# Tile pools change sides of the on-chip memory, and the state-space outputs move into the attention

## The chip, the cores and the metric

One core of one Trainium2 chip runs the whole program. The metric is the device time of one execution in microseconds (us); before the change it is 2275.36 us, the median of three runs that lie between 2270.74 and 2281.77 us. The profile was taken in one further execution.

## The reference

Two transformer blocks on 512 tokens of width 1024, all in float32. The first block has two layers. Layer 0 mixes with a windowed attention over the 512 tokens and 256 context tokens, layer 1 with a gated linear attention (GLA); each is followed by an MLP, `square(relu(h @ w_in)) @ w_out` with 4096 hidden columns. The second block projects `h` to q, k, v, a state-space input u and 2048 gate columns, and adds two branches:

```
gate   = sigmoid(proj[..., 3*D_ATTN+D_SSM:] + b_gate)
y_attn = chunked_relpos_attention(q, k, v, ...)        # 8 heads, causal within the 512 tokens
y_ssm  = s5_ssm_glu(u, ...)                            # scan; y = C s + D u; z = gelu(y)
                                                       # z * sigmoid(z @ w_glu + b_glu)
merged = gate[:, :, 0] * (y_attn @ wb[:D_ATTN]) + gate[:, :, 1] * (y_ssm @ wb[D_ATTN:])
x = x + merged @ w_out
x = x + hierarchical_moe(rms_norm(x), ...)             # 16 experts, top 2
```

## The kernel before, in words

**Products.** A float32 product is made of three float32r matmuls: each operand is split into a high part (a rounded copy, by ScalarE) and a rest (a subtraction, by VectorE), and high x high, high x rest and rest x high are added in PSUM. `Kern.unit` (L217) loads 1 MB of weights into a tile `raw` and splits it into `whi` and `wlo` (128 x 2048 each). `mm3s` (L248 to L252) writes the three matmuls. Of a matmul's two operands one is loaded into the array (stationary, 128 columns) and the other is streamed through it, here mostly 512 columns.

- `inproj` (L250 and its neighbours with `hl` in the profile's names): the weights are stationary, the activations `h` (high and rest, 16 KB per partition each) are streamed.
- The second half of `mlp` (`second`, names `hid`): the hidden activations are stationary, `whi` (lines L248 and L252) and `wlo` (L250) are streamed.
- `out_full` (names `oh`, `ol`): the weights are streamed, two units of them from `whi`/`wlo`, two from tiles `wr` of its own.

One MLP has 16 blocks of 256 hidden columns; each block has an `inproj` of 2 x 8 x 3 matmuls for each group of tokens, and a second part of 4 x 3 matmuls for each tile of 128 tokens. Layer 0 has a group of 512 tokens (`hl`) and one of 256 (`hc`), which alternate matmul by matmul; layer 1 has the 512 alone, and its first two blocks are cut into halves of 256 columns.

**Where tiles lie.** Pools are taken from two stacks: the left one grows upward from 16.1 KB of a partition's 224 KB, the right one downward from 224 KB. `Kern.left` and `Kern.right` go through `K.sides`, which can exchange the two. Before, the left stack begins with the constants (4.9 KB), the pool `wstream` (2 x `raw`, 2 x `whi`, 2 x `wlo`, 48 KB) and small scalars (1.1 KB). In the built program this puts `raw` at 21 to 37 KB, `whi` at 37 to 53 KB, `wlo` at 53 to 69 KB, the residual `X` at 70 to 86 KB, the MLPs' `hl` at 86 to 118 KB, and the block 2 input `h4` (its tiles are called `hl` too) at 127 to 159 KB. The hidden activations lie between 147 and 199 KB. In layer 0's `out_full`, `oh` and `ol` lie at 122 to 138 KB and `wr` at 138 to 170 KB.

**Order.** The Tile framework places each engine's instructions with a simulated timeline; the order in which the program emits them is its priority. In block 2 the emission is a set of Python generators (`block2_mix`, L1440): `scores(h)` yields after each of the four score tiles of a head, and at every second of these 32 steps one half of a gate unit (`gate_unit`, 24 matmuls with `h4` streamed, 16 halves in all) is emitted. `values` (the transposes of p and the products with V) of two heads follow during the next two heads. After the attention come, in this order: the loads of eight gate tiles, `ssm.load` (matrices G and W3, 2 MB each, W3 cut from DRAM in eight strided pieces), the first branch product (`ya`, 96 matmuls), in which `ssm.outputs` is emitted at two places, the GLU product (`z`, 48 matmuls), and the second branch product (`ys`). `ssm.outputs(Q)` computes a half of the state-space outputs: 16 matmuls with G and W3 for each of four `ii`, two copies, eight transposes, a gelu.

Of the kernel before, what the change touches and what calls it, by code (L numbers as in the profile page):

```python
# [19 lines left out]
P = 128  # L20
# [130 lines left out]
class Kern:  # L151
    def __init__(self, tc, A, at):
        self.tc, self.nc, self.A, self.at = tc, tc.nc, A, at
        self.stack = ExitStack()
        e = self.stack.enter_context
        self.c = e(tc.tile_pool(name="const", bufs=1))
        self.w = e(tc.tile_pool(name="wstream", bufs=2))
        self.s = None
        self.t = e(tc.tile_pool(name="tiny", bufs=6))
        self.dram = e(tc.tile_pool(name="dram", bufs=1, space=bass.MemoryType.DRAM))  # L160
        self.p2 = e(tc.tile_pool(name="ps2", bufs=2, space=bass.MemoryType.PSUM))
        self.p1 = e(tc.tile_pool(name="ps1", bufs=4, space=bass.MemoryType.PSUM))
        nc = self.nc


        self.ident = self.c.tile([P, P], F32, name="ident")
        self.identb = self.c.tile([P, P], BF, name="identb")
        self.csil = self.c.tile([P, KC, 32], F32, name="csil")
        self.small = self.c.tile([P, A["small"].shape[1]], F32, name="small")
        nc.sync.dma_start(self.small, A["small"])  # L170
        make_identity(nc, self.ident)
        nc.vector.tensor_copy(self.identb, self.ident)
        self.n = 0
        self.norms = []
        self.sides = {"left": "left", "right": "right"}
        edge = e(tc.tile_pool(name="edge", bufs=1, side="right"))
        self.mhalf = edge.tile([P, 8], F32, name="mhalf")
        self.edge_aff = edge.tile([P, 2, KC], F32, name="edge_aff")
        nc.vector.memset(self.mhalf, -0.5)
# [11 lines left out]

    def scratch(self, side="right"):

        st = ExitStack()
        self.s = st.enter_context(self.tc.tile_pool(name="scratch", bufs=1, side=side))
        return st
# [20 lines left out]
    def unit(self, ap, r=None, to=None, after=None, pool=False):  # L217

        r = self.raw(ap) if r is None else r
        hi, lo = to or (self.w.tile([P, 2048], F32R, tag="w" + x, name=self.nm("w" + x)) for x in ("hi", "lo"))  # L220
        ins = self.nc.scalar.copy(hi, r).ins  # L221
# [299 lines left out]
def layer0_attn(K):  # L521
# [11 lines left out]
    with ExitStack() as left:  # L533
        qp = left.enter_context(tc.tile_pool(name="qkv", bufs=1))
        Q = [qp.tile([P, NCTX + L], F32R, name=K.nm("Q")) for _ in range(16)]
# [301 lines left out]
def layer0(K):  # L837
# [26 lines left out]
    with K.scratch(), K.right("gate") as gp:  # L864
# [15 lines left out]
        mw, mw_close = K.opened(K.left("mw"))  # L880
        mlp(K, 0, list(h), [4, 2], finish2, swap, "right", filler=K.mod_dots(gp, mw), steps=4)
    K.ctx_close.close()
# [267 lines left out]
def layer1(K, X, h, ssm):  # L1150
# [16 lines left out]
    with K.scratch(), K.right("gate") as gp:  # L1167
# [13 lines left out]
        tp, t_close = K.opened(K.left("ssmt"))  # L1181
        mlp(K, 1, [h3], [4], finish2, swap, "right", True, ssm.constants(tp))
    return h


class SSM:


    def __init__(self, K):
        self.K = K  # L1190
        self.w1 = K.dram.tile([P, 2, 16, P], F32, name="ssm_w1")
        self.g = K.dram.tile([P, 2, 16, P], F32, name="ssm_g")
        self.k = K.dram.tile([16, 32, 15, 16], F32, name="ssm_k")
        self.a8 = K.c.tile([P, 2, 2, 16], F32, name="ssm_a8")

    def constants(self, tp):
# [149 lines left out]
        for q in range(8):  # L1346
            nc.gpsimd.dma_start(self.k.rearrange("c (a q) l x -> q c a (l x)", q=8)[q][:, :, 7 * 16:],
                                kk[16 * q:16 * q + 16])

    def inputs(self, zp, sp, u_rows):  # L1350

# [46 lines left out]

    def load(self, sp, between):

        nc = self.K.nc
        self.G = sp.tile([P, 2, 16, P], F32, name="ssm_g2", bufs=1)
        self.W3 = sp.tile([P, 32, P], F32, name="ssm_w3", bufs=1)
        for part in range(2):
            nc.sync.dma_start(self.G[:, part], self.g[:, part])
        between()
        for t in range(8):
            nc.sync.dma_start(self.W3[16 * t:16 * t + 16].rearrange("p g (t c) -> p g t c", t=8),
                              self.k[:, :, 7 - t:15 - t, :])

    def outputs(self, sp, Q, zT):

        K, Z, UT, G, W3 = self.K, self.Z, self.UT, self.G, self.W3
        nc, a, mm = K.nc, K.nc.scalar, K.nc.tensor.matmul
        b = [K.bank() for _ in range(2)]
        for ii in range(4):
# [8 lines left out]
            for g in range(2):  # L1425
                for i, o in os:
                    mm(o[g], UT[:, 2 * i + g, :], W3[:, 2 * i + g, :],
                       start=False, stop=True, skip_group_check=True)
        Y = sp.tile([P, 8, P], F32, tag="ssm_y", name=K.nm("Y"), bufs=1)
        for g, e in enumerate((a.copy, K.nc.vector.tensor_copy)):  # L1430
            e(Y.rearrange("p t (i g c) -> p g t i c", g=2, c=16)[:, g],
              b[g].rearrange("p (i t c) -> p t i c", i=4, t=8))
        b = K.bank2()
        for t in range(8):
            nc.tensor.transpose(b[:, t * P:t * P + P], Y[:, t, :], K.ident)
        for h in range(2):
            a.activation(zT[:, 2 * Q + h].rearrange("p (j t) -> p t j", t=8),
                         b.rearrange("p (t h j) -> p h t j", t=8, h=2)[:, h], AF.Gelu_apprx_tanh)


def block2_mix(K, X, hl, ssm, out):
# [6 lines left out]
    with ExitStack() as left:  # L1448
# [85 lines left out]

        with K.right("at2", 2) as ap:
            def scores(h):
# [57 lines left out]

            def gates(c0, c1):
                for c in range(c0, c1):
                    yield from gate_unit(c)

            last, done, gen = iter(()), [], gates(0, 8)
            for h in range(8):  # L1600
                for n, _ in enumerate(scores(h)):
                    if n % 2:
                        next(last, None)
                    else:
                        next(gen, None)
                if h % 2:
# [8 lines left out]
        z_close.close()  # L1615

        K.h_close.close()
        K.sides = {"left": "left", "right": "right"}
        K.opool = ExitStack()
# [22 lines left out]
        zs.push(sz_close)  # L1642
        gl = zs.enter_context(K.left("ssmz", 2))
        z = K.pair(gl, "z", [P, 4, L])
# [5 lines left out]

        with K.left("ssmr", 2) as sp:
            for r in range(4):
                fetch(r)
            ssm.load(sp, lambda: [fetch(r) for r in range(4, 8)])
            for c in range(2):
                w = K.unit(A["w_br"][c])
                for m in range(4):
                    f = 4 * c + m
                    b, g = branch(w, ya, m, f, f)
                    v.tensor_mul(mT[:, f, :], b, g)  # L1660
                    if c and m in (2, 3):
                        ssm.outputs(sp, m - 2, zT)
                        turned = parts(m - 2)
        yo = left.enter_context(K.left("b2o"))
# [38 lines left out]
class Moe:  # L1703
# [259 lines left out]
    def split(self, r):  # L1963
        K = self.K
        if self.nhi < 3:
            pool = self.more if self.nhi == 2 else K.w
            self.his.append([pool.tile([P, 2048], F32R, tag=t, name=K.nm(t)) for t in ("whi", "wlo")])
        hi, lo = self.his[self.nhi % 3]
# [118 lines left out]
def program(tc, A, at, out):  # L2087
# [3 lines left out]
    h = layer1(K, X, h, ssm)  # L2091
    K.sides = {"left": "right", "right": "left"}
    block2_mix(K, X, h, ssm, out).finish(X)
# [20 lines left out]
```

## Time and profile before

| | us |
|---|---|
| median of three runs | 2275.36 |
| the profiled execution's own time | 2268.23 |
| its span | 2266.2 |
| TensorE (PE) busy | 2138.9 (94%) |
| VectorE (DVE) busy | 1390.6 (61%) |
| ScalarE (ACT) busy | 971.2 (43%) |
| GpSimd (POOL) busy | 334.8 (15%) |
| TensorE's mean granted clock | 0.976 of full |

Busy time is a union of the records of one engine. Matmuls overlap in their records, since each record holds the pipeline's latency too: what one costs in a full stream is the distance from its start to the next one's start, which the timeline shows. "Idle before" in a row is the time that the engine stood still just ahead of the instruction, with what released it.

### The profile page before, as it was taken

The numbers are of one execution on the slowest core, as the hardware profiler recorded it, in microseconds if no ns is written. First come the engines' busy times: TensorE is split into PE (matmuls) and PEld (weight loads), VectorE is DVE, ScalarE is ACT, GpSimd is POOL, SyncE is SP. The second block draws the span as 40 slices with busy tenths as digits, with TensorE's granted clock in tenths as the row PEclk, the third lists the DMA queues.
The fourth block names the chain that finished last, engine by engine and source line by source line (L and its number), as shares of the span: only waits on it lengthen the run. The fifth ranks groups of instructions, "written<-read, shape, count | busy, mean of one in ns | idle before, by whom it ended". The sixth has DMA issues, their size and how long they took to land. (4 is left out here: it accounts for less than half of the span.)

```text
span 2266.2 us, 30706 instructions
## 1 busy us (share of the span) xinstructions
PE 2138.9 (94%) x12088; PEld 1769.3 (78%) x12088; DVE 1390.6 (61%) x2436; ACT 971.2 (43%) x1512; POOL 334.8 (15%) x453
## 2 busy tenths in 40 slices
PE   7999999999999999999989999999899997897996
PEld 5876668888888888789977887888799874686875
DVE  4666654999644444631794597555646754547985
ACT  5446656421121222542554632322353453535874
POOL 0035622112000000510000000000220100012332
PEclk9999999999999999999999999999999998998998
DMA  7112231557321121211211224232322435468993
GB/s 291 64 39 98 82 149 38 195 189 255 122 75 56 56 75 56 72 38 59 93 38 38 88 93 149 106 104 84 120 94 94 154 122 115 174 237 278 331 298 105
DMA packets 57970, 279.12 MB, mean 123 GB/s; under 512 B 9248, under 2 KB 13744, under 8 KB 32992
## 3 DMA queue, kind: packets, MB, share of 16 engines
q1 hardware_dynamic: 38048, 219.39, 27.4%
q0 software_dynamic: 18768, 55.04, 7.7%
q10 hardware_dynamic: 1008, 2.70, 0.4%
q8 instruction: 96, 1.57, 0.3%
q14 instruction: 50, 0.41, 0.1%
HBM read 264.54 MB, written 24.08 MB: 127 GB/s over the span
## 5 line engine op out<-in xcount | busy, mean ns | idle before, releaser
L221 ACT CAST whi<-raw 128x2048 fp32r<-128x2048 f32 x106 | 202.4, 1909 | 559.3 <-PE b L252 389.1
L222 DVE TENSOR_TENSOR wlo<-raw,whi 128x2048 fp32r<-128x2048 f32 x106 | 246.0, 2322 | 223.4 <-ACT whi L221 222.1
L250 PE MATMUL b<-hl,whi 128*128 128x512 f32 (+1 forms) x736 | 284.1, 386 | 2.3 <-DVE t L323 1.5
L248 PE MATMUL b<-hl,whi 128*128 128x512 f32 (+1 forms) x736 | 283.0, 385 | 0.8 <-ACT whi L221 0.8
L252 PE MATMUL b<-hl,wlo 128*128 128x512 f32 (+1 forms) x736 | 281.6, 386 | 0.0
L815 DVE TENSOR_TENSOR acc<-acc,b 128x512 f32<-128x512 f32 x280 | 180.8, 682 | 156.0 <-PE b L252 155.7
L248 PE MATMUL b<-whi,hid 128*128 128x512 f32 x640 | 215.5, 395 | 2.5 <-ACT whi L221 1.9
L250 PE MATMUL b<-wlo,hid 128*128 128x512 f32 x640 | 216.8, 394 | 0.0
L252 PE MATMUL b<-whi,hid 128*128 128x512 f32 x640 | 215.1, 395 | 0.0
L250 PEld LDWEIGHTS b<-hl,whi 128*128 128x128 f32 x736 | 139.1, 189 | 30.3 <-issue 2.9
L248 PEld LDWEIGHTS b<-hl,whi 128*128 128x128 f32 x736 | 139.1, 189 | 30.1 <-ACT whi L221 1.3
L252 PEld LDWEIGHTS b<-hl,wlo 128*128 128x128 f32 x736 | 139.3, 189 | 28.3 <-issue 0.2
L1970 DVE TENSOR_TENSOR wlo<-raw,whi 128x2048 fp32r<-128x2048 f32 x57 | 129.8, 2287 | 27.7 <-ACT whi L1970 27.7
L252 PEld LDWEIGHTS b<-whi,hid 128*128 128x128 f32 x640 | 120.3, 188 | 27.9
L248 PEld LDWEIGHTS b<-whi,hid 128*128 128x128 f32 x640 | 119.2, 188 | 29.0 <-ACT whi L221 2.1
L250 PEld LDWEIGHTS b<-wlo,hid 128*128 128x128 f32 x640 | 120.5, 188 | 27.4
L1970 ACT CAST whi<-raw 128x2048 fp32r<-128x2048 f32 x57 | 108.4, 1912 | 10.7 <-PE b L242 10.6
L627 POOL TENSOR_TENSOR p<-p,t 128x512 f32<-128x512 f32 (+2 forms) x96 | 92.5, 972 | 62.8 <-DVE t L626 62.2
L402 DVE CUSTOM_DVE_ANT_0 junk<-mw,cb 128x1024 bf16<-128x1024 f32 x80 | 97.6, 1220 | 3.6 <-DMA mw<-in_w_modT_dram 2.9
L240 PE MATMUL b<-whi,hl 128*128 128x256 f32 x320 | 91.3, 285 | 2.3 <-ACT qr L1478 2.3
L241 PE MATMUL b<-wlo,hl 128*128 128x256 f32 x320 | 91.4, 286 | 0.0
L242 PE MATMUL b<-whi,hl 128*128 128x256 f32 x320 | 91.2, 285 | 0.0
(602 smaller groups left out, 4709.8 us busy)
## 6 DMA issues: line engine op xcount, KB each, us to landing
raw<-in_w_e_dram SPq DMA_DIRECT2D x57, 1024.0 KB, 7.0
raw<-in_w_mlp_in_dram SPq DMA_DIRECT2D x32, 1024.0 KB, 5.1
raw<-in_w_mlp_out_dram SPq DMA_DIRECT2D x32, 1024.0 KB, 4.7
mw<-in_w_modT_dram POOLq DMA_DIRECT2D x56, 512.0 KB, 4.5
raw<-in_w_mod_dram SPq DMA_DIRECT2D x20, 1024.0 KB, 6.3
raw<-in_w_in_dram SPq DMA_DIRECT2D x16, 1024.0 KB, 4.8
raw<-in_gla_in_dram SPq DMA_DIRECT2D x12, 1024.0 KB, 4.8
raw<-in_w_o_dram SPq DMA_DIRECT2D x8, 1024.0 KB, 4.7
```

Source lines behind the costliest of these rows:

```text
L221: ins = self.nc.scalar.copy(hi, r).ins
L222: ins = ins, (self.nc.gpsimd if pool else self.nc.vector).tensor_sub(lo, r, hi.bitcast(F32)).ins
L240: mm(out, ah, bh, start=start, stop=False)
L241: mm(out, ah, bl, start=False, stop=False)
L242: mm(out, al, bh, start=False, stop=stop)
L248: mm(o, ah, b, start=start, stop=False)
L250: mm(o, ah, b, start=False, stop=False)
L252: mm(o, al, b, start=False, stop=stop)
L402: v.tensor_tensor_reduce(junk, w, cb[b], 1.0, 0.0, ALU.mult, ALU.add, to[:, k, b:b + 1])
L627: nc.gpsimd.tensor_mul(p[:, :n], p[:, :n], den.to_broadcast([P, n]))
L815: nc.vector.tensor_add(a, a, bs[n])
L1970: ins = K.nc.scalar.copy(hi, r).ins, K.nc.vector.tensor_sub(lo, r, hi.bitcast(F32)).ins
```

## The change

The permanent pools go to the right stack in a new order, `whi` and `wlo` get pools of their own, and every `left` and `right` of the three phases is exchanged. In block 2 the state-space outputs become a generator that fills steps of the attention after the gates; the fill is advanced at every step of the scores, not at every second one. Their matrices G and W3 are loaded once the gates are done; W3 is laid out ahead in DRAM by eight GpSimd DMAs (`k8`) at the end of layer 1's preparation, so that it comes in one load. Their scratch tile Y is taken from the `whi` pool, and the transposes and gelus are cut in two. The split of `zT` (`parts`) moves to the first unit of the first branch.

```diff
@@ Kern.__init__
-        self.c = e(tc.tile_pool(name="const", bufs=1))
-        self.w = e(tc.tile_pool(name="wstream", bufs=2))
+        edge = e(tc.tile_pool(name="edge", bufs=1, side="right"))
+        self.w = e(tc.tile_pool(name="wstream", bufs=2, side="right"))
+        self.c = e(tc.tile_pool(name="const", bufs=1, side="right"))
+        self.t = e(tc.tile_pool(name="tiny", bufs=6, side="right"))
+        self.wsplit = {x: e(tc.tile_pool(name=f"w{x}", bufs=2, side="right")) for x in ("lo", "hi")}
-        self.sides = {"left": "left", "right": "right"}
+        self.sides = {"left": "right", "right": "left"}
@@ unit
-        hi, lo = to or (self.w.tile([P, 2048], F32R, tag="w" + x, name=self.nm("w" + x)) for x in ("hi", "lo"))
+        hi, lo = to or (self.wsplit[x].tile([P, 2048], F32R, tag="w" + x, name=self.nm("w" + x)) for x in ("hi", "lo"))
@@ layer0, layer1 (both calls of mlp)
-        mlp(K, 0, list(h), [4, 2], finish2, swap, "right", ...)
+        mlp(K, 0, list(h), [4, 2], finish2, swap, "left", ...)
@@ SSM.constants
+        for t in range(8):
+            nc.gpsimd.dma_start(self.k8[16 * t:16 * t + 16].rearrange("p g (t c) -> p g t c", t=8),
+                                self.k[:, :, 7 - t:15 - t, :])
@@ SSM.load
-        between()
-        for t in range(8):
-            nc.sync.dma_start(self.W3[16 * t:16 * t + 16].rearrange("p g (t c) -> p g t c", t=8),
-                              self.k[:, :, 7 - t:15 - t, :])
+        nc.sync.dma_start(self.W3, self.k8)
@@ SSM.outputs
-        b = [K.bank() for _ in range(2)]
...
+            yield
-        Y = sp.tile([P, 8, P], F32, tag="ssm_y", name=K.nm("Y"), bufs=1)
+        Y = K.wsplit["hi"].tile([P, 2048], F32, tag="whi", name=K.nm("Y"))[:, :1024].rearrange("p (t c) -> p t c", t=8)
...
+        yield
+        for x in range(2):
+            for t in range(4):
+                nc.tensor.transpose(b[x][:, t * P:t * P + P], Y[:, 4 * x + t, :], K.ident)
+            for h in range(2):
+                a.activation(zT[:, 2 * Q + h].rearrange("p (j t) -> p t j", t=8)[:, 4 * x:4 * x + 4],
+                             b[x].rearrange("p (t h j) -> p h t j", t=4, h=2)[:, h], AF.Gelu_apprx_tanh)
+        yield
@@ block2_mix
-        with K.right("at2", 2) as ap:
+        sr = ExitStack()
+
+        def ssm_outputs():
+
+            K.h_close.close()
+            ssm.load(sr.enter_context(tc.tile_pool(name="ssmr", bufs=1, side=K.sides["right"])))
+            for Q in range(2):
+                yield from ssm.outputs(gbank, Q, zT)
+
+        with K.left("at2", 2) as ap:
...
+            def fill():
+                for c in range(8):
                     yield from gate_unit(c)
+                yield from ssm_outputs()
...
                     if n % 2:
                         next(last, None)
-                    else:
-                        next(gen, None)
+                    next(gen, None)
...
-        with K.left("ssmr", 2) as sp:
-            for r in range(4):
-                fetch(r)
-            ssm.load(sp, lambda: [fetch(r) for r in range(4, 8)])
...
-                    if c and m in (2, 3):
-                        ssm.outputs(sp, m - 2, zT)
-                        turned = parts(m - 2)
+        for r in range(8):
+            fetch(r)
...
+                if c == 0 and m < 2:
+                    turned = parts(m)
@@ program
-    K.sides = {"left": "right", "right": "left"}
+    K.sides = {"left": "left", "right": "right"}
     block2_mix(K, X, h, ssm, out).finish(X)
```

## Rows read from the trace of the kernel before

**Rows 1.** The profile's page, its first line.

```profile
span 2266.2 us, 30706 instructions
```

**Rows 2.** Busy time by stretch: PE, PEld, DVE, ACT, POOL (instructions), clock, DMA share, GB/s.

```profile
395.00:1043.00 648.00, 635.46 (x3357) 543.19 (x3356) 389.40 (x565) 187.36 (x298) 69.85 (x85) 0.99 0.31 106
...
1258.00:1642.00 384.00, 372.66 (x1781) 306.81 (x1780) 251.15 (x376) 129.13 (x163) 26.56 (x32) 0.99 0.31 107
...
1755.00:1861.00 106.00, 106.00 (x500) 83.98 (x500) 71.56 (x220) 52.41 (x94) 9.68 (x22) 1.00 0.39 134
1861.00:1898.00 37.00, 30.30 (x134) 17.02 (x132) 22.19 (x69) 17.43 (x42) 0.74 (x2) 0.86 0.12 43
1898.00:1957.00 59.00, 45.26 (x326) 34.04 (x325) 17.70 (x18) 28.30 (x32) 0.00 (x0) 0.91 0.70 172
```

**Rows 3.** Groups by line and form, PE: one of three MLP second-part lines.

```profile
L250 PE MATMUL b<-wlo,hid 128*128 128x512 f32 x640 | 216.8, 394 | 0.0
```

**Rows 4.** Timeline of PE in layer 1's MLP: start us, us, instruction, count.

```profile
1326.79 0.39 PE L248 MATMUL b<-hl,whi 128*128 128x512 f32 x1
...
1333.76 0.40 PE L252 MATMUL b<-hl,wlo 128*128 128x512 f32 x1
...
1343.75 0.39 PE L248 MATMUL b<-whi,hid 128*128 128x512 f32 x1
...
1349.32 0.39 PE L250 MATMUL b<-hl,whi 128*128 128x512 f32 x1
```

**Rows 5.** Timeline of PE in block 2's gates, `h4` streamed.

```profile
1781.80 0.39 PE L252 MATMUL b<-hl,wlo 128*128 128x512 f32 x1
...
1790.19 0.39 PE L248 MATMUL b<-hl,whi 128*128 128x512 f32 x1
```

**Rows 6.** Timeline of PE in layer 0's `out_full`, one tile of tokens.

```profile
337.25 0.62 PE L252 MATMUL b<-whi,ol 128*128 128x512 f32 x2
...
341.91 0.63 PE L248 MATMUL b<-wr,oh 128*128 128x512 f32 x2
342.38 0.62 PE L250 MATMUL b<-wr,oh 128*128 128x512 f32 x2
...
347.37 0.62 PE L248 MATMUL b<-whi,oh 128*128 128x512 f32 x2
```

**Rows 7.** Timeline of PE after the attention: the state-space outputs and the waits around.

```profile
1917.84 1.12 PE L1423 MATMUL b<-ssm_g,ssm_z 64*64 64x128 f32 x8 [5.74 <-DVE mT L1660]
...
1929.15 0.66 PE L1427 MATMUL b<-ssm_w,ssm_ut 128*64 128x128 f32 x8 [4.19 <-DMA ssm_w<-ssm_k]
...
1940.63 0.66 PE L1427 MATMUL b<-ssm_w,ssm_ut 128*64 128x128 f32 x8
...
1946.69 1.03 PE L1435 MATMUL b<-ident,Y 128*128 128x128 f32 x8
...
1951.00 1.19 PE L248 MATMUL b<-z,whi 128*128 128x512 f32 x4 [1.90 <-ACT z L1648]
...
1957.42 0.73 PE L248 MATMUL b<-ys,whi 128*128 128x512 f32 x2 [0.33 <-ACT ys L1676]
```

**Rows 8.** Timeline of ACT in the attention's end and after it.

```profile
1864.48 1.27 ACT L1545 CAST KH<-kT 64x512 fp32r<-64x512 f32 x2
...
1875.84 1.24 ACT L1545 CAST KH<-kT 64x512 fp32r<-64x512 f32 x2
...
1898.05 0.59 ACT L1592 CAST ya<-b 128x512 fp32r<-128x512 f32 x1 [4.13 <-PE b L1585]
...
1916.34 0.72 ACT L1637 ACTIVATE g<-g,small 128x512 f32<-128x512 f32 x1 [9.84 <-DMA g<-gates_d]
...
1936.77 1.28 ACT L1437 ACT_TABLE_LOAD   x1
```

**Rows 9.** Timeline of POOL in layer 1's MLP.

```profile
1515.55 4.06 POOL L1347 DMA_DIRECT2D ssm_k<-ssm_kk  x8 [82.96 <-ACT hf L755]
1612.74 4.62 POOL L222 TENSOR_TENSOR ya<-raw,ya 128x2048 fp32r<-128x2048 f32 x1 [93.13 <-ACT ya L221]
```

More of the change, by code (lines that the diff above doesn't have):

```diff
@@ L155, in __init__ @@
         e = self.stack.enter_context
-        self.c = e(tc.tile_pool(name="const", bufs=1))
-        self.w = e(tc.tile_pool(name="wstream", bufs=2))
+        edge = e(tc.tile_pool(name="edge", bufs=1, side="right"))
[3 more added lines that the diff above has]
+        self.wsplit = {x: e(tc.tile_pool(name=f"w{x}", bufs=2, side="right")) for x in ("lo", "hi")}
         self.s = None
-        self.t = e(tc.tile_pool(name="tiny", bufs=6))
         self.dram = e(tc.tile_pool(name="dram", bufs=1, space=bass.MemoryType.DRAM))
@@ L174, in __init__ @@
         self.norms = []
-        self.sides = {"left": "left", "right": "right"}
-        edge = e(tc.tile_pool(name="edge", bufs=1, side="right"))
+        self.sides = {"left": "right", "right": "left"}
         self.mhalf = edge.tile([P, 8], F32, name="mhalf")
@@ L190, in opened, with scratch @@
         return st.enter_context(pool), st
-    def scratch(self, side="right"):
+    def scratch(self, side="left"):
         st = ExitStack()
@@ L533, in layer0_attn @@
     with ExitStack() as left:
-        qp = left.enter_context(tc.tile_pool(name="qkv", bufs=1))
+        qp = left.enter_context(K.left("qkv"))
         Q = [qp.tile([P, NCTX + L], F32R, name=K.nm("Q")) for _ in range(16)]
@@ L880, in layer0 @@
         mw, mw_close = K.opened(K.left("mw"))
-        mlp(K, 0, list(h), [4, 2], finish2, swap, "right", filler=K.mod_dots(gp, mw), steps=4)
+        mlp(K, 0, list(h), [4, 2], finish2, swap, "left", filler=K.mod_dots(gp, mw), steps=4)
     K.ctx_close.close()
@@ L1181, in layer1 @@
         tp, t_close = K.opened(K.left("ssmt"))
-        mlp(K, 1, [h3], [4], finish2, swap, "right", True, ssm.constants(tp))
+        mlp(K, 1, [h3], [4], finish2, swap, "left", True, ssm.constants(tp))
     return h
@@ L1193, in __init__ @@
         self.k = K.dram.tile([16, 32, 15, 16], F32, name="ssm_k")
+        self.k8 = K.dram.tile([P, 32, P], F32, name="ssm_k8")
         self.a8 = K.c.tile([P, 2, 2, 16], F32, name="ssm_a8")
@@ L1397, in ahead, with load @@
         self.us = [K.unit(W[6 + i], to=[flat(x) for x in t], pool=i == 0) for i, t in enumerate((self.ya, (zT, UT)))]
-    def load(self, sp, between):
+    def load(self, sp):
         nc = self.K.nc
@@ L1405, in load, with outputs @@
             nc.sync.dma_start(self.G[:, part], self.g[:, part])
-        between()
-        for t in range(8):
-            nc.sync.dma_start(self.W3[16 * t:16 * t + 16].rearrange("p g (t c) -> p g t c", t=8),
-                              self.k[:, :, 7 - t:15 - t, :])
-    def outputs(self, sp, Q, zT):
+        nc.sync.dma_start(self.W3, self.k8)
+    def outputs(self, b, Q, zT):
         K, Z, UT, G, W3 = self.K, self.Z, self.UT, self.G, self.W3
         nc, a, mm = K.nc, K.nc.scalar, K.nc.tensor.matmul
-        b = [K.bank() for _ in range(2)]
         for ii in range(4):
@@ L1432, in outputs @@
               b[g].rearrange("p (i t c) -> p t i c", i=4, t=8))
[L1433 to L1438, printed above, removed]
+        yield
[6 more added lines that the diff above has]
+        yield
 def block2_mix(K, X, hl, ssm, out):
@@ L1593, in values @@
                 v.tensor_sub(ya[1][:, m, :], O, ya[0][:, m, :].bitcast(F32))
-            def gates(c0, c1):
-                for c in range(c0, c1):
+            def fill():
+                for c in range(8):
                     yield from gate_unit(c)
-            last, done, gen = iter(()), [], gates(0, 8)
+                yield from ssm_outputs()
+            last, done, gen = iter(()), [], fill()
             for h in range(8):
@@ L1615, in block2_mix @@
         z_close.close()
-        K.h_close.close()
-        K.sides = {"left": "left", "right": "right"}
+        sr.close()
+        K.sides = {"left": "right", "right": "left"}
         K.opool = ExitStack()
@@ L1642, in block2_mix @@
         zs.push(sz_close)
-        gl = zs.enter_context(K.left("ssmz", 2))
+        gl = zs.enter_context(K.right("ssmz", 2))
         z = K.pair(gl, "z", [P, 4, L])
@@ L1649, in parts @@
                     v.tensor_sub(z[1][:, d], zT[:, d], z[0][:, d].bitcast(F32)).ins)
-        with K.left("ssmr", 2) as sp:
-            for r in range(4):
-                fetch(r)
-            ssm.load(sp, lambda: [fetch(r) for r in range(4, 8)])
[L1655 to L1660, printed above, removed]
-                    if c and m in (2, 3):
-                        ssm.outputs(sp, m - 2, zT)
-                        turned = parts(m - 2)
+        for r in range(8):
+            fetch(r)
+        for c in range(2):
+            w = K.unit(A["w_br"][c])
+            for m in range(4):
+                f = 4 * c + m
+                b, g = branch(w, ya, m, f, f)
+                v.tensor_mul(mT[:, f, :], b, g)
+                if c == 0 and m < 2:
+                    turned = parts(m)
         yo = left.enter_context(K.left("b2o"))
@@ L1965, in split @@
         if self.nhi < 3:
-            pool = self.more if self.nhi == 2 else K.w
-            self.his.append([pool.tile([P, 2048], F32R, tag=t, name=K.nm(t)) for t in ("whi", "wlo")])
+            self.his.append([(self.more if self.nhi == 2 else K.wsplit[t]).tile([P, 2048], F32R, tag="w" + t,
+                                                                                name=K.nm("w" + t)) for t in ("hi", "lo")])
         hi, lo = self.his[self.nhi % 3]
```

## The prediction

> **What bounds the kernel now.** The span is 2266.2 us [rows 1]; the profiled execution took 2268.23 us and the median of three runs is 2275.36, so whatever is summed here against the profile is put on the median, 7.1 us higher. I read busy time by stretch first. In both MLPs PE is busy for all but 13 of 648 and 11 of 384 us, and VectorE and the DMA queues have room: 60 to 65% busy, and a DMA share of 0.31 [rows 2]. There a time can only fall if each matmul costs less. The gates' stretch is full too: 106 of 106 us. Then PE goes loose: 30.3 us of 37 in the attention's end and 45.3 of 59 behind it, at a mean clock of 0.86 and 0.91 of full, between its two levels of 1.2 and 2.4 GHz [rows 2]. The change has one part for each kind of stretch.
>
> **Part one, the places.** A matmul's cost in a full stream is read from start to start. In layer 1's MLP 31 with `hl` streamed start in 6.97 us (30 steps, 232.3 ns) and 24 with `whi` and `wlo` streamed take 5.57 us (232.1 ns) [rows 4]. In the gates 38 with `h4` streamed start in 8.39 us (37 steps, 226.8 ns) [rows 5]. Both `hl` runs have the same shapes, the same line, and `whi`/`wlo` as the stationary operand; what differs is that `hl` lies at 86 to 118 KB and `h4` at 127 to 159 KB. The best contrast is inside one loop: in `out_full` 20 matmuls that stream `whi`/`wlo` (37 to 69 KB) take 4.66 us, 233.0 ns each, and 22 that stream `wr` (138 to 170 KB) take 4.99 us, 226.8 ns, with the same stationary tiles [rows 6]. So a 512-column matmul costs 5.5 ns less when its streamed operand lies in the upper part. Why, no row shows.
>
> The Trainium skill ("TensorE: Matmul & The Clock Gate", section "Wait — 56ns, not 53.3ns?") has the distance from start to start as the columns over 2.4 GHz plus about 2.5 ns, 215.7 ns for 512 columns, wherever the operand lies. The trace disagrees twice, in size and in the two paces; by the page part one would be worth nothing.
>
> The new places follow from the stack. From 224 KB down: `raw` 16, constants 4.9, scalars 1.1, `wlo` 16, `whi` 16, `X` 16, `hl` 32. So `wlo` lies at 186 to 202 KB, `whi` at 170 to 186, the MLPs' `hl` at 122 to 154; in block 2 `X`, 24 KB of `ya`/`zT` and 16.6 KB of state-space tiles put `h4` at 81 to 113. Terms, at 5.5 ns:
> - `whi` streamed in the MLPs' second parts: two of three lines of 640 [rows 3], 1280 x 5.5 = -7.0 us.
> - `wlo`: 640, above every place that rows 4 to 6 show as quick: between 0 and -3.5; I take -1.8.
> - Layer 1's `hl`: 16 x 2 x 8 x 3 = 768, less 192 cut into 256 columns: 576 x 5.5 = -3.2.
> - Layer 0's `hl`: 768, each followed by a 256-column one, a pair for which no row stands: 0 to -4.2; I take -1.0.
> - The gates lose their place: 16 x 24 = 384 x 5.5 = +2.1.
> - `out_full` gains for `whi` what it loses for `wr`; the experts and the branches go both ways: 0, by at most 1.5 either way (some 300 matmuls).
>
> That is -10.9; a run that is broken up need not keep the quick pace, so I take **-9**, with ends -14 and +4 (the losses alone).
>
> **Part two, the state-space outputs.** From the last head's output (1898.05) [rows 8] to the first matmul of `ys` (1957.42) [rows 7] lie 59.4 us. PE is busy for 45.3 us of them [rows 2]. What goes: the state-space matmuls, nearly all between 1929.15 and 1941.3, 12 us, 8 transposes at 1946.69 (1.0), and the waits. The 5.74 us that PE stood before 1917.84 is put down to `mT`, and that one waited for a sigmoid whose gate tile arrived only at 1916.34, 9.84 us late, its DMA between those of G and W3 [rows 8]; the 4.19 us before 1929.15 is W3 itself; the 1.90 before 1951.00 is the split of the second half of `zT` [rows 7]. So 45.3 - 13 = 32.3 us of work stay, `ya` and `z`; a mean clock of 0.91 over the stretch says that a few of these ran at 1.2 GHz, and I take 3 off. 59.4 - 29.3 = **-30 us**.
>
> What comes back in the attention:
> - Its own end. The gates now come at every step. If the scores keep to their emission, only four heads are done when the gates run out, where the trace has five, and a head without cover takes 11.4 us (the K copies of two heads at 1864.48 and 1875.84 [rows 8]); less its matmuls that moved, about +8 to +13. If the framework starts scores when they are ready, as now, 0. I take +6.
> - The 13 us of matmuls fall into idle time: 37 - 30.3 = 6.7 us [rows 2], about as much again with one more head. What doesn't fit: +3 (0 to 6).
> - Gelu stands among exponentials. One table load is 1.28 us [rows 8]; two groups of gelus give up to four more loads and spare one, 5.1 - 1.3 us on ScalarE, which is half idle: +3 (0 to 4).
> - The first branch shares its banks with the outputs and can start less early: +1 (0 to 3).
>
> The Trainium skill ("ScalarE: Activation LUTs", section "What ACT_TABLE_LOAD costs") has about 2.7 us for a load; the row has 1.28. By the page this term would be up to +8 and the sum 5 us worse.
>
> At nothing: the eight `k8` DMAs. POOL has no work between the `ssm_k` writes at 1515.55 (0.5 us each) and 1612.74, 93 us [rows 9], and 2 MB beside a DMA share of 0.31 [rows 2] delay nobody; without that cover they would cost POOL some 5 us. The loads of G and W3 start when `h4` is free and have the attention's end as cover; if that is too short, see the third rival. The moved `parts` (1 us on ACT, 1.2 on DVE each) lie beside `ya`.
>
> Sum of part two: -30 + 6 + 3 + 3 + 1 = **-17**, ends -28 and -4. Both parts: 2268.2 - 26 = 2242 on the profile, 2249 on the median.
>
> **Rivals.**
> 1. *The place counts for nothing* (the skill's rule, or a cause that only looks like a place, such as which pool was written last). For it: no row shows a mechanism. Against it: rows 6 change pace in one loop, with one stationary operand. Then only -17 is left: 2258.
> 2. *Everything falls well*: the attention ends where it did, `wlo` is quick too. -14 - 28: 2234. For it: in the trace gates and scores were not tied to their emission.
> 3. *The new operands come late*: PE takes its queue in order, so a state-space matmul that waits for G or W3 holds the scores behind it, and these the exponentials. 4 MB at the 172 GB/s of rows 2 need 24 us. Held for 12 us, part two gives -5 and the sum is 2261, or 2266 with half of part one: no change.
> 4. *Slower*: the same hold at its full 24 us, with its price added to heads that are themselves without cover (+13 and the 7 for tables and banks): -30 + 24 + 13 + 7 = +14, 2289, or 2280 if part one holds. It decides from the point at which hold and longer attention exceed the 30 us taken away, and is slower only if the places give nothing. Against it: the simulated timeline sets what it expects to be late further back in the queue.
>
> **How the numbers follow.** 0.5% is 11.4 us, about what a measurement of this kernel can tell from no change. The forecast has 0.50, the first rival 0.18, the second 0.10, the third 0.14, the fourth 0.08. Forecast and first two are faster, but a first rival with a longer attention is not (0.02 off): faster 0.76, same 0.16, slower 0.08. The range takes in the second rival's time and the third's, and leaves out the fourth: 2233 to 2271.
>
> **What would show it.** Right: in layer 1's MLP, `hl` and `whi` runs near 227 ns from start to start, and the two MLP stretches some 7 and 4 us shorter; `wlo` decides the disputed 3.5. The gates at 232. No L1423 or L1427 after the last `ya` copy, no wait of PE for `mT` or W3 there, and 27 to 32 us from that copy to the first `ys`. The last copy itself 0 to 20 us later, counted from the gates' start. Wrong: MLP runs still at 232 (first rival); a wait of L1423 or L1427 for a DMA with scores behind it (third and fourth); a PE that is idle by more than 20 us in the attention's end; or a stretch outside these that grows, since all pools have new neighbours, and a tile's first write waits for whoever lay there before.

## The result and the profile after

The changed kernel takes 2247.41 us, the median of four runs (2239.76 to 2248.39), against 2273.53 for the kernel before, the median of four (2270.74 to 2281.77): a ratio of 0.9877, with a 95% interval of 0.9858 to 0.9896. It is faster by 26 us, 1.2%. The forecast was 2249, its range 2233 to 2271. The profiled execution took 2239.76 us, span 2237.9, 28.3 less than the span of before [rows 1]; the other three runs are about 8 us longer, so its trace is used for stages only.

Busy time by stretch, with the columns of [rows 2] (PE, PEld, DVE, ACT, POOL, clock, DMA share, GB/s), of the changed kernel:

```profile
395.00:1041.00 646.00, 632.11 (x3348) 542.10 (x3349) 388.59 (x564) 185.97 (x295) 68.83 (x84) 0.99 0.31 106
1258.00:1635.00 377.00, 364.71 (x1781) 305.99 (x1780) 250.87 (x376) 129.81 (x165) 30.62 (x40) 0.99 0.33 115
...
1848.00:1908.00 60.00, 48.84 (x379) 31.26 (x378) 33.16 (x96) 38.90 (x76) 0.83 (x3) 0.97 0.32 119
1908.00:1935.00 27.00, 26.64 (x117) 21.70 (x117) 18.34 (x19) 21.07 (x26) 0.00 (x0) 1.00 0.72 254
```

The attention's end now takes 60 us where it took 37, the chain behind it 27 where it took 59, and PE's clock there is 0.97 and 1.00 where it was 0.86 and 0.91 [rows 2].

How long an MLP takes is read best from one line's first and last start: the matmuls that stream `wlo`, in layer 0's MLP (x384) and in layer 1's (x256). Instructions by line, the kernel before:

```profile
L250 PE MATMUL b<-wlo,hid x384: 390/392/479, 432.6 to 942.4; 128*128 128x512 f32 x192
...
L250 PE MATMUL b<-wlo,hid x256: 387/393/404, 1290.1 to 1632.8; 128*128 128x512 f32 x128
```

The same view of the changed kernel:

```profile
L253 PE MATMUL b<-wlo,hid x384: 387/389/478, 432.3 to 939.1; 128*128 128x512 f32 x192
...
L253 PE MATMUL b<-wlo,hid x256: 389/389/402, 1291.1 to 1626.5; 128*128 128x512 f32 x128
```

Timeline of the changed kernel: a run of `hl` and one of `whi`/`wlo` in layer 1's MLP, one tile of layer 0's `out_full`, the gates (their first matmul; then a run), the first `ys`, and the last matmuls of the program:

```profile
336.60 0.62 PE L255 MATMUL b<-whi,ol 128*128 128x512 f32 x2
...
341.13 0.62 PE L251 MATMUL b<-wr,oh 128*128 128x512 f32 x2
...
346.57 0.62 PE L251 MATMUL b<-whi,oh 128*128 128x512 f32 x2
...
1326.90 0.39 PE L251 MATMUL b<-hl,whi 128*128 128x512 f32 x1
...
1333.70 0.39 PE L255 MATMUL b<-hl,wlo 128*128 128x512 f32 x1
1333.93 1.07 PE L251 MATMUL b<-whi,hid 128*128 128x512 f32 x4
...
1339.37 0.39 PE L251 MATMUL b<-hl,whi 128*128 128x512 f32 x1
...
1747.13 0.39 PE L251 MATMUL b<-hl,whi 128*128 128x512 f32 x1
...
1774.13 0.39 PE L255 MATMUL b<-hl,wlo 128*128 128x512 f32 x1
...
1781.10 0.39 PE L255 MATMUL b<-hl,wlo 128*128 128x512 f32 x1
...
1934.80 0.62 PE L251 MATMUL b<-ys,whi 128*128 128x512 f32 x2
...
2226.11 0.63 PE L255 MATMUL b<-whi,g 128*128 128x512 f32 x2
```

Against [rows 4]: 31 matmuls with `hl` in 6.80 us, 30 steps of 226.7 ns (232.3 before); 24 with `whi` and `wlo` in 5.44 us, 226.7 (232.1 before); the gates 31 in 6.97 us, 232.3 (226.8 before, [rows 5]). So far this is as forecast. `out_full` is not: its 20 matmuls with `whi`/`wlo` take 226.5 ns each and its 24 with `wr` 226.7, although `wr` now lies at 86 to 118 KB, where `hl` was slow before.

Where the 28.3 us of the two spans went:

| from ... to | before | after | difference |
|---|---|---|---|
| start, first `wlo` of layer 0's MLP | 432.6 | 432.3 | -0.3 |
| to its last `wlo` | 509.8 | 506.8 | -3.0 |
| to the first `wlo` of layer 1's MLP | 347.7 | 352.0 | +4.3 |
| to its last `wlo` | 342.7 | 335.4 | -7.3 |
| to the first gate matmul | 122.5 | 120.6 | -1.9 |
| to the last `ya` copy (the attention) | 142.8 | 160.5 | +17.7 |
| to the first `ys` | 59.4 | 27.2 | -32.2 |
| to the program's last matmuls | 290.0 | 291.3 | +1.3 |
| to the end of the span | 18.7 | 11.8 | -6.9 |

The last line is one that the forecast does not have.

### The profile page after: what moved, and what is told of

The parts are those of the page before. It is cut to its first block, busy times and chain, and to the rows that moved or that the text cites. A ratio compares the mean times of both kernels' runs of the same rounds, so it can differ in the third digit from the quotient of the medians.

```text
span 2237.9 us, 30692 instructions
## 1 busy us (share of the span) xinstructions
PE 2121.2 (95%) x12088; PEld 1766.9 (79%) x12088; DVE 1391.0 (62%) x2436; ACT 975.6 (44%) x1520; POOL 335.5 (15%) x461
## 3 DMA queue, kind: packets, MB, share of 16 engines
q0 software_dynamic: 19408, 57.14, 8.1%
## 5 line engine op out<-in xcount | busy, mean ns | idle before, releaser
L251 PE MATMUL b<-whi,hid 128*128 128x512 f32 x640 | 213.4, 392 | 3.1 <-ACT whi L224 1.9
L255 PE MATMUL b<-whi,hid 128*128 128x512 f32 x640 | 211.7, 390 | 0.0
L243 PE MATMUL b<-whi,hl 128*128 128x256 f32 x320 | 91.3, 285 | 2.3 <-ACT qr L1485 2.3
L626 DVE CUSTOM_DVE_ANT_0 p<-b,mask,nsink 128x512 f32<-128x512 f32 (+2 forms) x96 | 67.5, 704 | 38.6 <-PE b L622 25.6
```

The lines of the kernel that those rows point to most:

```text
L243: mm(out, ah, bh, start=start, stop=False)
L251: mm(o, ah, b, start=start, stop=False)
L255: mm(o, al, b, start=False, stop=stop)
L626: nc.vector.tensor_tensor_reduce(p[:, :n], S[:, a0:a0 + n], added[:, z:z + n], -1.0, ns, ALU.add, ALU.min, nmx)
```

## What else `wr` and `whi` differ in

The tiles' start addresses can be read from the built programs, and they give another reading of the two paces. What counts would be how the start addresses of a matmul's two operands stand against each other modulo 256 bytes (below: their *phase*), not how high the streamed one lies. Remainders modulo 256:

| | before | after |
|---|---|---|
| `whi`, `wlo` | 0 | 128 |
| `hl`, `hc`, `hid`, `oh`, `ol`, `wr` | 128 | 128 |
| `h4` (gates) | 0 | 0 |
| phase in both MLPs | 128 | 0 |
| phase in the gates | 0 | 128 |
| phase of `whi` / `wr` in layer 0's `out_full` | 128 / 0 | 0 / 0 |

This fits every pace above, `out_full`'s too. The phase turned because the pool of small scalars, 1152 bytes (4.5 x 256), lay between the weight pools and the rest before and does not now. The height and the phase can be told apart by moving that pool alone.

## Experiments on the places

**The pool of small scalars, moved in the kernel before.**

```diff
+        self.t = e(tc.tile_pool(name="tiny", bufs=6))
         self.w = e(tc.tile_pool(name="wstream", bufs=2))
         self.s = None
-        self.t = e(tc.tile_pool(name="tiny", bufs=6))
```

> The kernel before with one line moved: the pool of small scalars (1152 bytes) is created ahead of the weight stream's pool, so raw, whi and wlo lie 1152 bytes higher and nothing else moves. All heights stay as before (whi and wlo at 38 to 70 KB, the MLPs' hl at 86 to 118 KB). Theory A, the height (as predicted): nothing changes, 2273 us +-3, MLP runs of 512 columns at 232 ns from start to start. Theory B, the phase (the two operands' start addresses against each other, modulo 256 bytes: 128 in the MLPs before, 0 after the change): the phase in both MLPs becomes 0 as in the changed kernel and these runs go to 227 ns; MLP of layer 1 about 7 us shorter, MLP of layer 0 about 2 to 3, out_full and w_out about 1, while the gates (phase 128 now) go from 227 to 232 ns and lose 2: about 2265 us in all (2262 to 2268).

Measured: 2265.04 us against 2273.06, ratio 0.9960 (0.9943 to 0.9977). Instructions by line, then the timeline of layer 1's MLP:

```profile
L250 PE MATMUL b<-wlo,hid x384: 387/389/478, 433.1 to 939.9; 128*128 128x512 f32 x192
...
L250 PE MATMUL b<-wlo,hid x256: 389/389/402, 1291.2 to 1626.3; 128*128 128x512 f32 x128
```

```profile
1326.98 0.39 PE L248 MATMUL b<-hl,whi 128*128 128x512 f32 x1
...
1333.78 0.39 PE L252 MATMUL b<-hl,wlo 128*128 128x512 f32 x1
```

The run of 31 takes 6.80 us, 226.7 ns, with `hl` still at 86 to 118 KB. The gates, whose `h4` did not move either, go the other way, from 226.8 to 232.7 ns (31 matmuls from 1775.38 to 1782.36). The MLPs take 506.8 and 335.1 us, as in the changed kernel. One moved line has all of part one.

**The same pool, moved in the changed kernel.**

```diff
-        self.t = e(tc.tile_pool(name="tiny", bufs=6, side="right"))
         self.wsplit = {x: e(tc.tile_pool(name=f"w{x}", bufs=2, side="right")) for x in ("lo", "hi")}
+        self.t = e(tc.tile_pool(name="tiny", bufs=6, side="right"))
```

> The changed kernel with one line moved: the pool of small scalars is created behind the pools of whi and wlo, so these lie 1152 bytes higher (171 to 203 KB) and nothing else moves. Theory A, the height: nothing changes, 2247 us +-3, MLP runs at 227 ns. Theory B, the phase: it becomes 128 in both MLPs and 0 in the gates; MLP runs go back to 232 ns, the gates to 227; about 2256 us (2253 to 2259).

Measured: 2250.81 us, ratio to the kernel before 0.9895 (0.9875 to 0.9915).

```profile
L253 PE MATMUL b<-wlo,hid x384: 390/392/479, 433.9 to 943.8; 128*128 128x512 f32 x192
...
L253 PE MATMUL b<-wlo,hid x256: 390/393/404, 1291.9 to 1634.8; 128*128 128x512 f32 x128
```

```profile
1328.66 0.39 PE L251 MATMUL b<-hl,whi 128*128 128x512 f32 x1
...
1335.63 0.40 PE L255 MATMUL b<-hl,wlo 128*128 128x512 f32 x1
```

The run is back at 6.97 us (232.3 ns) with `hl` at 122 to 154 KB and `whi` above 170, and the MLPs at 509.9 and 342.9 us; the gates are at 226.7 ns (31 matmuls from 1783.62 to 1790.42). So the stage speaks for the phase as clearly as before; the total, 3.4 us above the changed kernel's, is less than the 9 expected and its interval overlaps the other one. Of what the MLPs lose, the stretch between them gives back 3.9 us (348.1 for the changed kernel's 352.0). With the run before, pace and height are separated in both directions: the height is worth nothing here.

**Each part alone.** Both kernels are put together from lines of the two: `pools_only` has the pools and sides of the change and block 2 of before, `ssm_only` the reverse.

```diff
-        self.c = e(tc.tile_pool(name="const", bufs=1))
-        self.w = e(tc.tile_pool(name="wstream", bufs=2))
+        edge = e(tc.tile_pool(name="edge", bufs=1, side="right"))
+        self.w = e(tc.tile_pool(name="wstream", bufs=2, side="right"))
...
+        self.wsplit = {x: e(tc.tile_pool(name=f"w{x}", bufs=2, side="right")) for x in ("lo", "hi")}
```

> The kernel before with the changed kernel's pools alone (part one). Forecast: 9 us off, 2264 (2260 to 2268). By the trace of the changed kernel: about 7 us in the MLP of layer 1, 2 to 3 in that of layer 0, 2 back in the gates. Rival, that the pools give nothing: 2273.

> The changed kernel's order of block 2 (part two) on the pools of before. If the two parts simply add, part two alone takes 17 to 20 us off: 2253 to 2257. Forecast theory: the chain from the last ya copy to the first ys falls from 59 to about 28 us, the attention's end is some 6 to 10 us later. Rival: the end of the attention pays more without the other pools (at2 lies elsewhere), and only about 10 us are left: 2263.

Measured: 2265.52 us (ratio 0.9969, 0.9953 to 0.9985) and 2252.33 us (0.9906, 0.9884 to 0.9928), beside 2273.06. That is -7.5 and -20.7; together -28.3, where both parts in one kernel have -26.1. The parts add within what the runs can tell. Part two is better by 4 us than forecast, although its stretch is not: in `ssm_only` first gate matmul to first `ys` takes 187.5 us, as in the changed kernel (187.7), 14.6 less than before. The rest is the last line of the table, below.

**Phase 0 in the gates and the experts.** Three unused tiles shift `h4`, `ys` and the experts' operands.

```diff
+        self.sz.tile([P, 32], F32, name="pad_b2s", bufs=1)
...
+        one("pad_moe", [P, 40])
...
+        one("pad_moes", [P, 24])
```

> The changed kernel with three unused tiles of 128, 160 and 96 bytes in pools of block 2 and of the experts, so that the phase (start addresses of streamed and stationary operand against each other, modulo 256 bytes) is 0 also in the gates, the second branch, w_out2 and the experts. Phase theory: the gates go from 232 to 227 ns (384 matmuls, 2.0 us), w_out2's and the experts' runs from 233 to 227; 2 to 5 us less, 2242 to 2245. Height theory: h4 still lies at 81 to 113 KB, nothing changes, 2247.

Measured: 2243.89 us, ratio 0.9884 (0.9863 to 0.9905). Timeline of the gates:

```profile
1773.84 0.39 PE L255 MATMUL b<-hl,wlo 128*128 128x512 f32 x1
...
1780.64 0.39 PE L255 MATMUL b<-hl,wlo 128*128 128x512 f32 x1
```

The same 31 gate matmuls take 6.80 us instead of 6.97, with `h4` at 81 to 113 KB: the phase a third time. The runs of `w_out2` and of the experts that stood at a phase of 96 go from medians of 232 to 235 ns to 227. In the total nothing can be told from the changed kernel: the intervals of the ratios overlap, and from the first gate matmul to the first `ys` only 0.8 us is gained.

**The pairs of layer 0.**

```diff
+    hp.tile([P, 32], F32, name="pad_h1l")
     h[0] = K.pair(hp, "hl", [P, KC, L])
```

> The changed kernel with an unused tile of 128 bytes between layer 0's hl and hc, so that in layer 0's MLP the phase of hl against the weights stays 0 and that of hc becomes 128. A pair (512 columns with hl, 256 with hc) took 350 to 351 ns with both at 128 (before) and 352 to 353 with both at 0 (changed kernel). Theory A: each matmul keeps the pace that its own phase has in a run of its kind, 227 + 120 = 347: 768 pairs, some 4 us off layer 0's MLP, 2243. Theory B: the change of the streamed length breaks the pace whatever the phase: 350 to 353, no change.

Measured: 2241.48 us, ratio 0.9865 (0.9831 to 0.9899). 34 pairs of layer 0's MLP in the timeline of the changed kernel and, in the second fence, of this one; the last row is the first one behind them:

```profile
689.30 0.39 PE L251 MATMUL b<-hl,whi 128*128 128x512 f32 x1
...
701.30 0.63 PE L251 MATMUL b<-whi,hid 128*128 128x512 f32 x2
```

```profile
687.27 0.39 PE L251 MATMUL b<-hl,whi 128*128 128x512 f32 x1
...
699.07 0.63 PE L251 MATMUL b<-whi,hid 128*128 128x512 f32 x2
```

A pair costs 353 ns in the changed kernel and 347 here (351 in the same 34 pairs of the kernel before, both at 128). Theory A holds, and the MLP is 3.4 us shorter: its `wlo` line goes from 431.8 to 935.2 us.

**All phases together.** The tiles of the last two kernels in one.

> The changed kernel with the unused tiles of both earlier variants together: phase 0 in the gates, the second branch, w_out2 and the experts, and hc at 128 against hl at 0 in layer 0's MLP. Phase theory: layer 0's MLP 3.5 us shorter than in the changed kernel (pairs at 347 ns), the gates 2 us shorter; the experts, beside a DMA share of 0.81, give little or nothing: 2241 us (2239 to 2244), ratio to the kernel before 0.985. Rival: the gains are lost again in the attention's end and the experts, 2247.

Measured: 2242.54 us, ratio 0.9867 (0.9844 to 0.9891). Layer 0's MLP again takes 503.4 us on its `wlo` line. The median is 5 us under the changed kernel's, but the runs of the kernel before that were taken beside it were 3 us faster as well (2270.09 for 2273.53); the intervals of the ratios overlap, and what is shown is the 3.4 us in the MLP's rows.

## Experiments on the state-space outputs

**W3 without k8.** The eight GpSimd DMAs go, and W3 is cut from DRAM in the attention, as before.

```diff
-        nc.sync.dma_start(self.W3, self.k8)
+        for t in range(8):
+            nc.sync.dma_start(self.W3[16 * t:16 * t + 16].rearrange("p g (t c) -> p g t c", t=8),
+                              self.k[:, :, 7 - t:15 - t, :])
```

> The changed kernel without k8: W3 is again loaded in eight strided pieces, now in the attention. Theory A (the tail belongs to the eight GpSimd DMAs): the tail goes back to 13.2 us, +6. Beyond that, theory C: W3 comes later by 3 to 8 us, the state-space matmuls wait for it at the head of PE's queue and hold the scores behind them; 2255 to 2260 in all. Rival D: the state-space matmuls have slack and the load's form is worth nothing beside the tail: 2253.

Measured: 2266.78 us, ratio 0.9970 (0.9953 to 0.9986): some 20 us more than the changed kernel, and more than C had. Timeline of SP's queue and of PE:

```profile
1849.80 14.80 SPq L1410 DMA_DIRECT2D ssm_w<-ssm_k  x8
...
1859.00 0.71 PE L1424 MATMUL b<-ssm_g,ssm_z 64*64 64x128 f32 x8 [2.74 <-DMA ssm_g<-ssm_g]
...
1874.75 1.12 PE L1428 MATMUL b<-ssm_w,ssm_ut 128*64 128x128 f32 x8 [9.56 <-DMA tb<-in_rel_dram]
```

And the same places in the changed kernel:

```profile
1848.57 0.43 SPq L1414 DMA_DIRECT2D ssm_w<-ssm_k  x1
...
1856.23 0.51 PE L1427 MATMUL b<-ssm_g,ssm_z 64*64 64x128 f32 x8 [1.21 <-DMA ssm_g<-ssm_g]
...
1862.52 0.66 PE L1431 MATMUL b<-ssm_w,ssm_ut 128*64 128x128 f32 x8 [0.70 <-DMA ssm_w<-ssm_k]
```

The eight pieces hold SP's queue for 14.8 us, where one load takes 0.43, and PE stands 9.56 us at the first matmul with W3 (its wait is put down to a later transfer of the same queue, `tb`), with the scores behind it. This is the hold of the prediction's third rival, and it came as soon as k8 was gone. In the profiles the last `ya` copy comes 178.4 us after the first gate matmul, 17.9 later than in the changed kernel; some 6 more of the 20 us are the tail of the next experiment, which is as long here as in the kernel before. The rival, worked out from that kernel, had 2261 to 2266, and 2266.8 is measured. With k8 the waits are 1.21 and 0.70 us.

**Where the tail comes from.** From the end of the last scatter to the end of the span the kernel before takes 13.2 us, the changed one 7.5. Two kernels add GpSimd DMAs to the kernel before at k8's place, whose results nothing reads: k8 itself, and eight DMAs of 512 bytes.

```diff
+        for t in range(8):
+            nc.gpsimd.dma_start(self.k8[16 * t:16 * t + 16].rearrange("p g (t c) -> p g t c", t=8),
+                                self.k[:, :, 7 - t:15 - t, :])
```

```diff
+        for t in range(8):
+            nc.gpsimd.dma_start(self.k8[t:t + 1, 0, :], self.k[t:t + 1, 0, 0:8, :].rearrange("c l x -> c (l x)"))
```

> The kernel before with the eight GpSimd DMAs that write the new layout of W3 (k8) added at the end of layer 1's preparation; nothing reads what they write. It tests where 6 us of the changed kernel come from that the prediction did not have: from the end of the last scatter to the end of the span the four kernels with these DMAs take 7.5 us and the kernels without them 13.2. Theory A, these DMAs themselves (161 instead of 153 DMAs issued by GpSimd): the tail falls to about 7.5 us, 2267 us in all. Theory B, something of the moved outputs: the tail stays at 13.2 and the time at 2273. Both theories: they delay nothing in layer 1's MLP, which keeps 344 us from its first to its last second-part matmul.

> The kernel before with eight GpSimd DMAs of 512 bytes each at the place of k8's (153 becomes 161 issued by GpSimd, nothing reads what they write). Theory A: the tail behind the last scatter hangs on the number of DMAs that GpSimd has issued: 7.5 us instead of 13.2, 2267 us. Theory B: it hangs on the 2 MB and the many packets of k8: the tail stays at 13.2, 2273.

Measured: k8 alone 2268.09 us against 2275.07, ratio 0.9970 (0.9957 to 0.9983); the small ones 2271.36 against 2271.7, 0.9997 (0.9978 to 1.0017). First the span, GpSimd's DMA queue and the last scatter of the kernel with k8 alone, then those of the kernel with the small DMAs:

```profile
span 2268.2 us, 30721 instructions
...
q0 software_dynamic: 19408, 57.14, 8.0%
...
2259.07 1.55 POOL L2019 DMA_INDIRECT out_dram<-xy,tab  x1 [3.86 <-DMA out_dram<-x,tab]
```

```profile
span 2276.6 us, 30717 instructions
...
q0 software_dynamic: 19024, 55.05, 7.5%
...
2261.82 1.55 POOL L2018 DMA_INDIRECT out_dram<-xy,tab  x1 [3.93 <-DMA out_dram<-x,tab]
```

With k8 the tail is 2268.2 - 2260.6 = 7.6 us; with the small ones it is 2276.6 - 2263.4 = 13.2, as before. So k8's DMAs bring these 6 us, and not by their number. The trace's raw records show where: the last DRAIN instruction of GpSimd takes 6.20 us with the small ones, as before, and 1.54 with k8. Of the fourteen kernels profiled here the five with 19024 packets or fewer in that queue end with 13.1 to 13.3 us; of the nine with 19408 eight end with 7.2 to 7.6 and the one without the gelu (below) with 5.0. Whether the packets' count or the bytes decide, and why, is open.

**The fill's pace.** The fill is advanced at every second step again.

```diff
                     if n % 2:
                         next(last, None)
-                    next(gen, None)
+                    else:
+                        next(gen, None)
```

> The changed kernel with the fill advanced at every second step of the scores, as the gates were before, so that the state-space outputs are emitted only behind the last scores. The attention's end (first gate matmul to last ya copy) was 142.8 us before and 160.5 after. Theory E (as predicted): part of these 17.7 us is lost cover, heads without gates beside them; with the slower fill the last copy comes 8 to 12 us earlier, while the outputs, 13 us of matmuls, fall behind it into the first branch: 2247 to 2255 in all. Rival F: the framework places by readiness, the two emissions give the same order: 2247 +-2.

Measured: 2242.8 us, ratio 0.9870 (0.9849 to 0.9892), not to be told from the changed kernel. Timeline of ACT, the last `ya` copy:

```profile
1909.19 0.59 ACT L1608 CAST ya<-b 128x512 fp32r<-128x512 f32 x1 [5.42 <-PE b L1601]
```

It comes 161.7 us after the first gate matmul (1747.53), no earlier than the 160.5 of the changed kernel: the gain that theory E expected does not come. The price of lost cover is not settled by this. The edit does give the cover back: the last gate matmul starts 106.9 us after the first one (100.2 in the changed kernel, 105.3 before), the last K copies after 120.8 us (135.3, 120.5). But the state-space matmuls come later with it: the last one with W3 starts at 1895.08, which is 147.6 us after the first gate matmul, for 132.4. From the first gate matmul to the last `ya` copy, in the columns of [rows 2], the kernel before, the changed one, this one:

```profile
1755.30:1898.05 142.75, 136.05 (x630) 100.75 (x629) 93.49 (x288) 69.84 (x135) 10.42 (x24) 0.96 0.32 111
```

```profile
1747.13:1907.59 160.46, 149.30 (x838) 110.97 (x837) 94.72 (x290) 82.53 (x151) 10.04 (x24) 0.99 0.35 125
```

```profile
1747.53:1909.19 161.66, 156.88 (x838) 114.15 (x837) 95.29 (x290) 78.40 (x148) 10.16 (x24) 0.94 0.34 122
```

PE is idle for 4.8 us here, where it is idle for 11.2 in the changed kernel and for 6.7 before; but it is busy for 7.6 us longer than in the changed kernel, at a mean clock of 0.94 for 0.99.

**Without the gelu.**

```diff
-                a.activation(zT[...], b[x]..., AF.Gelu_apprx_tanh)
+                a.copy(zT[...], b[x]...)
```

> The changed kernel with the eight gelus of the state-space outputs replaced by plain copies of the same tiles (z is then y itself: the gelu is left out). A copy needs no activation table of its own, so the six table loads between 1868 and 1890 us go. Theory A: the table loads (four more than before, 1.28 us each) and the exponentials that wait behind them are part of the 17.7 us by which the attention's end came later; it comes 3 to 6 us earlier, 2242 to 2245. Theory B: the 17.7 us are the state-space matmuls themselves and PE's waits, ScalarE has room: no change, 2247 +-2.

Measured: 2245.26 us, ratio 0.9887 (0.9853 to 0.9921). Timeline of ACT, of the changed kernel first:

```profile
1868.26 1.28 ACT L1443 ACT_TABLE_LOAD   x1
...
1889.53 1.28 ACT L1579 ACT_TABLE_LOAD   x1
...
1907.59 0.59 ACT L1608 CAST ya<-b 128x512 fp32r<-128x512 f32 x1 [4.10 <-PE b L1601]
```

```profile
1907.65 0.59 ACT L1608 CAST ya<-b 128x512 fp32r<-128x512 f32 x1 [5.21 <-PE b L1601]
```

All six table loads are gone and the last copy comes 161.2 us after the first gate matmul (1746.50), as in the changed kernel. The same stretch of this kernel:

```profile
1746.50:1907.65 161.15, 154.58 (x838) 114.25 (x837) 94.74 (x290) 74.26 (x146) 10.13 (x24) 0.95 0.35 124
```

The time is the one that theory B gives, but not for its reason alone: without the loads PE is idle for 6.6 us instead of 11.2, and its matmuls take 5.3 us longer, at a clock of 0.95 for 0.99. So leaving the gelu out gains nothing; that the loads cost nothing at an equal clock is not shown.

## Why the prediction was right, and where it was not

**The total.** 2247.4 for 2249, but two terms were wrong in opposite senses: the longer attention was too small by 6 us (12 for 17.7), and 6 us at the end of the program were not foreseen. That the sum came within 2 us is luck. Two of its sums are off by a little: by its own terms the lower end of part two is -30, not -28, and -14 - 28 on the median gives 2233 for the second rival, not 2234. Neither changes the forecast.

**Part one: the size was right, the reason wrong.** The failed step is the reading of [rows 6]: "a 512-column matmul costs 5.5 ns less when its streamed operand lies in the upper part". `wr` and `whi` differ in height and in phase, and the height was taken. The 5.5 ns and the count of matmuls held by luck, since the new pools, which the prediction judged by height, give the MLPs phase 0 as well. The first rival names "a cause that only looks like a place"; that cause exists, but the change turns it too, so 2258 did not come. Term by term:
- `whi` in the second parts and layer 1's `hl`: 226.7 ns, as forecast. `wlo`, taken at half, has it in full; the MLP of layer 1 is 7.3 us shorter, "some 7" was forecast.
- Layer 0's `hl` (-1.0): a pair costs 353 ns for 351, 768 x 2 ns = +1.6. Both phases became 0, and the pairs want `hc` at 128. The MLP still has -3.0, for "some 4"; by the paces alone, 1152 second-part matmuls at -5.5 ns and the pairs, it would be -4.7, and the rest is open.
- The gates: 232.3, as forecast. `out_full`: `wr` loses nothing.
- +4.3 us between the two MLPs was not foreseen. The kernel with the moved scalars has 1291.2 - 939.9 = 351.3 there against 347.7, and the changed kernel with the scalars moved last 348.1, so it comes and goes with the phase; its causes were not separated.

Of the Trainium skill's rule cited in the prediction ("TensorE: Matmul & The Clock Gate", section "Wait — 56ns, not 53.3ns?", 215.7 ns for 512 columns) no run shows the figure: these float32r matmuls have 226.7 ns at their best phase.

**Part two.** The chain behind the attention: -30 forecast, -32.2 measured, 27.2 us long, with a clock of 1.00; no state-space matmul and no wait for `mT` or W3 is left in it. The attention's end: +6, +3 and +3 for lost cover, matmuls without room and table loads, +17.7 measured. Neither the slower fill nor the missing tables bring any of it back, but in both runs the clock is lower, so neither term has a price of its own. The step that failed is "the 13 us of matmuls fall into idle time": they lengthen the stretch almost in full. By the rows above PE is busy for 149.3 us in it where it was 136.1, and idle for 11.2 where it was 6.7: +13.2 and +4.5 are the 17.7. The state-space matmuls and transposes take some 14 us there, read from start to start; 28 matmuls of the first branch lie in it before and after. This is an account of one trace of each kernel; what the +4.5 waits for was not isolated.

The 2.7 us that the prediction takes from the Trainium skill ("ScalarE: Activation LUTs", section "What ACT_TABLE_LOAD costs") stand there for a whole switch of tables, the load and a drain of the engine; for the load alone the page has 1283 ns, as the rows do (1.28 us). In this trace a whole switch takes hardly longer: 1.31 us from the end of the copy before the load at 1868.26 to the start of the gelu behind it.

**k8** was costed at nothing, and rightly: in the kernel with k8 alone layer 1's MLP takes 344.0 us from its first to its last second-part matmul, 343.9 before. What the step left out is its worth: without it the third rival's hold is the result, and the end of the program is some 6 us longer. With the one load that the change has, neither the third rival nor the fourth came.

## What to carry to other kernels

Before a pace is put down to where a tile lies, list both operands' start addresses: here 1152 bytes between two pools set whether 512-column float32r matmuls ran at 227 or at 232 ns, and moving one line gave 8 us. When work is moved into a stretch that waits in order, prepare its operands in the layout of one plain load first: with the eight strided loads nearly all that the move gave was gone again. Busy shares say little on what fits into idle time; count the idle time again afterwards.

## What the runs showed of the hardware

- The pace of a float32r matmul of 512 columns depends on the two operands' start addresses against each other modulo 256 bytes: 226.7 ns at 0 and 232.3 at 128, in runs without a break, whichever of the two is moved and at every height from 38 to 202 KB that the runs had; 96 has 232 to 235. Other phases were not compared. For pairs of 512 and 256 columns the best of three settings is 0 and 128 (347 ns). No run shows why.
- 2 MB more through GpSimd's DMA queue, some 700 us earlier, make the program's end 5.7 us shorter (GpSimd's last DRAIN instruction takes 1.54 us for 6.20); eight small DMAs do not. Why is open.
- Eight strided loads of 256 KB hold the issuing queue for 14.8 us, one of 2 MB for 0.43.
- With and without six activation table loads of 1.28 us among the exponentials the attention ended at the same place (161.2 us without them, 160.5 with them), at a clock of 0.95 without and 0.99 with them. So their own cost is not shown.
